# Two of eleven pairs of inner tiles multiplied directly instead of through seven block products

## The chip, the cores and the metric

The kernel runs on one core of a Trainium2 chip. The metric is the device time of one execution in microseconds (us), from a few runs, of which the median is given. TensorE (PE in the rows) multiplies, VectorE (DVE), ScalarE (ACT) and GpSimd (POOL) work element by element, and SyncE (SP) issues the transfers.

## What is computed

A decoder trunk of two layers on 512 tokens of width 1024, all in float32. Every layer is two feed-forward networks (FFNs) around a mixer; the mixers (convolution with sparse attention, short convolution with stick-breaking attention) are not touched by the change. D_FF is 2816.

```python
def _rmsnorm(x, g):
    y = x32 * lax.rsqrt(jnp.mean(x32 * x32, axis=-1, keepdims=True) + RMS_EPS)
    return (y * g.astype(jnp.float32)).astype(x.dtype)

def _swiglu(x, w_in, w_out):
    gate, up = jnp.split(x @ w_in, 2, axis=-1)
    return (jax.nn.silu(gate) * up) @ w_out

def reference(x, ...):
    for layer in range(DEPTH):
        x = x + 0.5 * _swiglu(_rmsnorm(x, ffn1_norm[layer]), ffn1_w_in[layer], ffn1_w_out[layer])
        h = _rmsnorm(x, mix_norm[layer])
        ...
        x = x + y
        x = x + 0.5 * _swiglu(_rmsnorm(x, ffn2_norm[layer]), ffn2_w_in[layer], ffn2_w_out[layer])
    return _rmsnorm(x, final_norm)
```

## The kernel before

The residual `xT` is kept transposed: 8 tiles of 128 channels by 512 tokens. A float32 operand is **split** (`split`, L85) into a high part (ScalarE) and a rest (VectorE, the subtraction), and each product of two split operands is three matmuls (`mm3`, L117 to L120: high x high, high x rest, rest x high). The 2816 inner channels are 22 tiles of 128, taken as 11 **pairs**.

`up(s)` (L248) makes one pair: for each of its two tiles and for gate and up, `load_w` brings 512 KB of weights, splits them (three buffers each for the raw, the high and the rest part), and 24 matmuls of 512 columns fill a PSUM bank (`gu`, four banks with the tag `b`). VectorE multiplies the banks by `rstd`, ScalarE applies Silu, VectorE multiplies gate and up into `hb`. `Seven` (L135) then forms four sums of 256 columns (`ht`) and splits 1792 columns into `ah` and `al`: the seven operands of a Strassen-like 2x2 block product.

`down(c0, n, q, end)` (L270) multiplies n pairs with the output weights for one half (q) of the output tiles. `seven` (L210) loads four weight blocks (`rb`), builds weight sums (`ws`, L235, L236, L238, L242), and calls `product` seven times: a split of the weights, then 6n matmuls of 256 columns into one of the banks `px`, `py`, `pw` (there is one of each), then one update of two output tiles' halves of `xT` by VectorE (`taps`, L277). `px` and `pw` run on through several products of one call, so the update reads a bank between two products into it. `CHUNKS = [3, 3, 3, 2]` gives the number of pairs per call; `ffn` (L289 to L300) puts one `up` between the two halves of a chunk, ahead of need, so that the last chunk (2 pairs) has no `up` left beside it.

When the last chunk has updated four output tiles, `nxt(m)` is called for each: `Norm.add` (L171) makes the next phase's operands `xh` (ScalarE, L91) and `xl` (VectorE, L92), the square (ScalarE) and its running sum `ss` (POOL, the eighth on VectorE). `finish` sums over channels with one-column matmuls (`rs`), computes the inverse root in 12 small VectorE steps, and turns it into `rstd` (`rb`, L206, then ScalarE, L207). The matmuls of the next phase need `xh` and `xl`; its first eviction needs `rstd`. In the last FFN `nf_add` squares the first four tiles and scales them by the final gain, and `last(c, m0)` (L878) does the final norm for each half of the tokens: squares, gains (`xg`), row sums, transposes (`ft`, in banks of the tag `b`), outputs `o`.

The order of instructions on each engine is set when the program is built, by a scheduler with a timeline of its own, which follows the code's order as priority; each engine then runs its list in order.

The program runs FFN, mixer 0, FFN, FFN, mixer 1, FFN. After the first FFN mixer 0 begins with projections (banks `ac`), with windows `xw` that VectorE builds after `rstd`, their split `xwh`, and `cw` matmuls on them. The output projection of mixer 1 (`out_proj`, L362, banks `mo`) makes 24 matmuls, one update and one `nxt` per output tile.

Of the kernel before, what the change touches and what calls it, by code (L numbers as in the profile page):

```python
# [14 lines left out]
P = 128  # L15
# [18 lines left out]

S_11, S_21, S_22, S_T1, S_T3, S_T2, S_T4 = 1, 2, 3, 4, 5, 6, 7

CHUNKS = [3, 3, 3, 2]

FILL = [3, 1, 1, 2, 1, 1, 2, 1]

# [10 lines left out]
def trunk(ctx: ExitStack, tc: tile.TileContext, a: dict, out: bass.AP):  # L51
# [71 lines left out]
    def halves(t):  # L123
        return t.rearrange("p (s t) -> p s t", t=TH)
# [117 lines left out]
        V.tensor_tensor(s[2], s[2], raw["12"], ALU.add)  # L242
        product("3", X, s[2], S_22, False)

    def ffn(norm, w_in, w_out, nxt, ph, last=None):
        act = {}

        def up(s):  # L248

            blk = ph.wide("hb")  # L250
            for r in range(2):
                ps = []
                for gu in range(2):
                    hi, lo = load_w(w_in[2 * s + r, :, gu], KD * P)
                    o = ph.bank("gu")
                    for i, k in enumerate(norm.order):
                        sl = slice(k * P, (k + 1) * P)
# [12 lines left out]
        def down(c0, n, q, end):  # L270
# [18 lines left out]
        todo, done = [], 0  # L289
        for i, n in enumerate(CHUNKS):  # L290
            c0 = sum(CHUNKS[:i])

            while done < min(c0 + n + 1, NP // 2):
                up(done)
                done += 1
            for q in range(2):
                down(c0, n, q, i == len(CHUNKS) - 1)
                if done < NP // 2 and q == 0:
                    up(done)
                    done += 1  # L300

    def proj(norm, src, o, when=nullcontext):
        hi, lo = load_w(src, KD * P)
# [551 lines left out]

    with ffn_phase() as ph:
        n1.finish(lambda s: ph.bank(s, "n"))
        ffn(n1, a["w1_in"][0], a["w1_out"][0], n2.add, ph)
    with Phase(dict(q=8, t=5, p=3, d=4, cc=3), "ss", ss=3, pt=2, po=2, cv=1) as ph:
        n2.finish(lambda s: ph.bank(s, "po"))  # L860
        mixer0(n2, n3.add, ph)
    with ffn_phase() as ph:
        n3.finish(lambda s: ph.bank(s, "n"))
        n4 = Norm(P_N1 + 8)
        ffn(n3, a["w2_in"][0], a["w2_out"][0], n4.add, ph)
        n4.finish(lambda s: ph.bank(s, "n"))
        n5 = Norm(P_NM + 8)
        ffn(n4, a["w1_in"][1], a["w1_out"][1], n5.add, ph)
# [6 lines left out]
    def gain(m):  # L875
        return prm[:, P_NF + m:P_NF + m + 1]

    def last(c, m0):  # L878

        ts = slice(c * TH, (c + 1) * TH)  # L880
        parts = [nf.ss[0][:, ts]]
        xg = [xT[:, m, ts] for m in range(m0)]
        for m in range(m0, KD, 2):
            sq = ctile("sq")
            S.activation(halves(sq), xT[:, m:m + 2, ts], AF.Square)
            parts += [sq[:, :TH], sq[:, TH:]]
            x = ph.tile("xg")
            for j in range(2):
                xg.append(x[:, j * TH:(j + 1) * TH])
                V.tensor_scalar(xg[-1], xT[:, m + j, ts], gain(m + j), None, op0=ALU.mult)  # L890
# [21 lines left out]

    with ffn_phase() as ph:
        n6.finish(lambda s: ph.bank(s, "n"))
        ffn(n6, a["w2_in"][1], a["w2_out"][1], nf_add, ph, last)


def _layout(i):
# [12 lines left out]
    for s, t in (("1", "ffn1"), ("2", "ffn2")):  # L931
# [4 lines left out]
        w = i[f"{t}_w_out"].reshape(2, NP // 2, 2, P, 2, 2, 2, P).transpose(0, 4, 2, 5, 3, 6, 1, 7)  # L936
        cuts = np.split(w, np.cumsum(CHUNKS)[:-1], axis=6)
        w = np.concatenate([x.reshape(2, 2, 2, 2, P, -1) for x in cuts], axis=5)
        d[f"w{s}_out"] = c(w).reshape(2, 2, 4, P, NP * P)
# [76 lines left out]
```

## Time and profile before

| | |
|---|---|
| median of 3 runs | 1998.99 us (1998.45 to 1999.19) |
| the profiled execution, its own time | 1997.97 us |
| its span, first to last instruction | 1995.3 us |
| TensorE busy | 1942.7 us (97%) |
| VectorE busy | 1399.2 us (70%) |
| ScalarE busy | 809.5 us (41%) |
| GpSimd busy | 101.7 us (5%) |
| mean granted TensorE clock, share of full speed | 0.990 |

The profile shows one execution. Matmuls are pipelined and their ends are modelled, so two of them overlap in the rows: the rate is read from starts, not from durations. Full speed of the TensorE clock is 2.4 GHz, the lower level 1.2 GHz. A row of the timeline ends with the idle time of the engine before it and what it waited for.

### The profile page before, as it was taken

Reading aid. Unit: us, or ns where it says so; the run is one execution under the profiler, and the core shown is the slowest. Engines: PE = TensorE matmul, PEld = TensorE weight load, DVE = VectorE, ACT = ScalarE, POOL = GpSimd, SP = SyncE. Lnnn points to the kernel's source line nnn. Section 1 sums busy time; section 2 is a strip of 40 time slices with the busy share of each in tenths; the row PEclk is TensorE's granted clock in tenths of the full one; section 3 lists DMA queues with packets and bytes.
Section 4 is the critical chain, followed back from the end, with each engine's and each line's share of the span. In section 5 each row is a group of like instructions: output and inputs, shape, how many; then the busy total and the mean of one; then the engine's idle time right before and its main releaser. Section 6 shows DMA issues by size and latency. Waiting matters only on the chain.

```text
span 1995.3 us, 26109 instructions
## 1 busy us (share of the span) xinstructions
PE 1942.7 (97%) x10428; PEld 1649.8 (83%) x10428; DVE 1399.2 (70%) x2114; ACT 809.5 (41%) x1173; POOL 101.7 (5%) x109
## 2 busy tenths in 40 slices
PE   8999999889999999999989999998999999999998
PEld 6898988768667888898877888888877888888897
DVE  6575757799976656675786666668758755676667
ACT  5343333436785333333343333334645433333333
POOL 2000000100332100000010000000000010000000
PEclk9999999999999999999989999999999999999999
DMA  6233332222101432333233333331321243232311
GB/s 219 90 98 93 98 102 71 79 87 85 43 1 42 133 102 84 107 90 101 82 91 106 93 101 102 96 91 31 107 74 53 85 135 99 87 110 82 115 45 59
DMA packets 56280, 178.07 MB, mean 89 GB/s; under 512 B 6240, under 2 KB 6624, under 8 KB 56160
## 3 DMA queue, kind: packets, MB, share of 16 engines
q1 hardware_dynamic: 56016, 176.29, 29.1%
q8 instruction: 81, 1.33, 0.3%
q14 instruction: 39, 0.32, 0.0%
q10 hardware_dynamic: 144, 0.14, 0.0%
HBM read 174.30 MB, written 2.10 MB: 88 GB/s over the span
## 4 chain that ended last, share of the span: by engine, by line
PE 93%; DVE 4%; ACT 1%; issue 1%; DMA 1%; SPq 0%; DVEq 0%; ACTq 0%
PE gu L118 16%; PE gu L119 16%; PE gu L120 16%; PE px L118 4%; PE px L119 4%; PE px L120 4%; PE ac L120 3%; PE ac L119 3%; PE ac L118 3%; PE pw L119 2%; PE pw L118 2%; PE pw L120 2%; PE mo L118 2%; PE mo L120 1%; PE mo L119 1%; PE pt L369 1%
## 5 line engine op out<-in xcount | busy, mean ns | idle before, releaser
L118 PE MATMUL gu<-xh,whi 128*128 128x512 f32 x1408 | 548.9, 391 | 11.4 <-ACT whi L88 7.6
L119 PE MATMUL gu<-xl,whi 128*128 128x512 f32 x1408 | 549.5, 390 | 0.1
L120 PE MATMUL gu<-xh,wlo 128*128 128x512 f32 x1408 | 545.2, 390 | 0.0
L88 ACT ACTIVATE whi<-raw 128x1024 fp32r<-128x1024 f32 (+2 forms) x240 | 251.8, 1050 | 563.5 <-PE gu L119 194.0
L89 DVE TENSOR_TENSOR wlo<-raw,whi 128x1024 fp32r<-128x1024 f32 (+2 forms) x240 | 291.0, 1214 | 50.6 <-ACT whi L88 48.7
L118 PEld LDWEIGHTS gu<-xh,whi 128*128 128x128 f32 x1408 | 265.0, 188 | 66.0 <-ACT whi L88 8.4
L120 PEld LDWEIGHTS gu<-xh,wlo 128*128 128x128 f32 x1408 | 264.6, 188 | 55.3
L119 PEld LDWEIGHTS gu<-xl,whi 128*128 128x128 f32 x1408 | 265.0, 188 | 54.2 <-DVE xl L92 1.0
L264 DVE TENSOR_TENSOR u<-gu,rstd 128x512 f32<-128x512 f32 x88 | 60.8, 691 | 262.0 <-PE gu L120 262.0
L88 ACT ACTIVATE whi<-rb 128x768 fp32r<-128x768 f32 (+1 forms) x128 | 101.5, 793 | 295.4 <-PE gu L119 166.3
L118 PE MATMUL px<-ah,whi 128*128 128x256 f32 x704 | 205.8, 292 | 11.6 <-DVE xT L277 9.3
L120 PE MATMUL px<-ah,wlo 128*128 128x256 f32 x704 | 201.2, 286 | 0.4 <-DVE wlo L89 0.4
L119 PE MATMUL px<-al,whi 128*128 128x256 f32 x704 | 200.6, 285 | 0.0
L261 DVE TENSOR_TENSOR g<-gu,rstd 128x512 f32<-128x512 f32 x88 | 60.8, 691 | 151.8 <-PE gu L120 145.7
L118 PEld LDWEIGHTS px<-ah,whi 128*128 128x128 f32 x704 | 134.7, 191 | 24.3 <-issue 8.9
L119 PEld LDWEIGHTS px<-al,whi 128*128 128x128 f32 x704 | 134.9, 192 | 1.0
L120 PEld LDWEIGHTS px<-ah,wlo 128*128 128x128 f32 x704 | 134.6, 191 | 0.7 <-DVE wlo L89 0.7
L120 PE MATMUL ac<-xh,wlo 128*128 128x512 f32 x288 | 113.7, 395 | 4.4 <-DVE wlo L89 4.4
L89 DVE TENSOR_TENSOR wlo<-rb,whi 128x768 fp32r<-128x768 f32 (+1 forms) x128 | 114.8, 897 | 0.8
L119 PE MATMUL ac<-xl,whi 128*128 128x512 f32 x288 | 114.0, 397 | 1.0 <-DVE xl L92 1.0
L118 PE MATMUL ac<-xh,whi 128*128 128x512 f32 x288 | 113.5, 395 | 1.1 <-ACT whi L88 0.9
L118 PE MATMUL pw<-ah,whi 128*128 128x256 f32 x352 | 100.7, 286 | 4.4 <-DVE xT L277 2.2
(307 smaller groups left out, 3179.5 us busy)
## 6 DMA issues: line engine op xcount, KB each, us to landing
raw<-in_w_in SPq DMA_DIRECT2D x174, 512.0 KB, 3.8
rb<-in_w_out SPq DMA_DIRECT2D x96, 384.0 KB, 3.1
raw<-in_cd_a SPq DMA_DIRECT2D x20, 512.0 KB, 3.6
rb<-in_w_out SPq DMA_DIRECT2D x32, 256.0 KB, 2.6
raw<-in_ab_a SPq DMA_DIRECT2D x16, 512.0 KB, 3.6
raw<-in_ab_w_out SPq DMA_DIRECT2D x8, 512.0 KB, 3.6
raw<-in_cd_w_out SPq DMA_DIRECT2D x8, 512.0 KB, 3.5
xT<-in_x SPq DMA_DIRECT2D x8, 256.0 KB, 5.8
```

Of the source, the lines that this page charges most:

```text
L88: S.activation(hi, src, AF.Copy)
L89: V.tensor_tensor(lo, src, hi, ALU.subtract)
L118: PE.matmul(o, wh, xh, start=start, stop=False, **kw)
L119: PE.matmul(o, wh, xl, start=False, stop=False, **kw)
L120: PE.matmul(o, wl, xh, start=False, stop=stop, **kw)
L261: V.tensor_tensor(g, ps[0], rstd, ALU.mult)
L264: V.tensor_tensor(u, ps[1], rstd, ALU.mult)
L369: PE.transpose(pt[:, w:w + P], src[:, OFFQ[i] + t * P:OFFQ[i] + (t + 1) * P], ident)
```

## The change

Only the first nine pairs go through `seven`, in three chunks of three. The last two pairs (four inner tiles, `TAIL = 4`) keep their natural element order and are split as they are (`at`, two tiles of 1024 columns) without sums. After the last chunk `down_tail` makes one output tile after the other: 12 matmuls of 512 columns into a bank `fo` of the tag `b` (four banks, shared with `gu`), one update of `xT`, then `nxt(m)`. One load and split of 1024 columns holds the weights of two output tiles. In the last FFN the eighth output tile is made in two halves of 256 tokens, and `last` squares and scales only this one. The host lays the tail's weights out as `w1_tail` and `w2_tail`. TensorE has 288 matmuls fewer in all: 672 of 256 columns go, 372 of 512 and 24 of 256 come, and 12 row sums go.

```diff
-CHUNKS = [3, 3, 3, 2]
+CHUNKS = [3, 3, 3]
+TAIL = NP - 2 * sum(CHUNKS)
...
-                V.tensor_tensor(o if r else o[:, ::-1], halves(g), halves(u), ALU.mult)
+                tail = s >= sum(CHUNKS)
+                V.tensor_tensor(o if r or tail else o[:, ::-1], halves(g), halves(u), ALU.mult)
+            if tail:
+                h, l = (ph.rtile("at", "act", 1792) for _ in range(2))
+                split(h[:, :1024], l[:, :1024], blk)
+                act[s] = [(h[:, r * T:(r + 1) * T], l[:, r * T:(r + 1) * T]) for r in range(2)]
+                return
...
-            if end and last and q == 1:
-                for c in range(2):
-                    last(c, m0)
-            elif end:
-                for m in range(m0, m0 + 4):
-                    nxt(m)
...
+        def down_tail(m, ts):
+            o = ph.bank("fo")[:, ts]
+            if m // 2 not in ws:
+                ws[m // 2] = load_w(w_tail[m // 2], 2 * TAIL * P)
+            hi, lo = ws[m // 2]
+            for k in range(TAIL):
+                sl = slice((m % 2 * TAIL + k) * P, (m % 2 * TAIL + k + 1) * P)
+                mm3(o, hi[:, sl], lo[:, sl], ops[k][0][:, ts], ops[k][1][:, ts], k == 0, k == TAIL - 1)
+            V.scalar_tensor_tensor(xT[:, m, ts], o, 0.5, xT[:, m, ts], op0=ALU.mult, op1=ALU.add)
+
+        cut = KD - 1 if last else KD
+        for m in range(cut):
+            down_tail(m, slice(0, T))
+            nxt(m)
+        if last:
+            for c in range(2):
+                for m in range(cut, KD):
+                    down_tail(m, slice(c * TH, (c + 1) * TH))
+                last(c, range(cut, KD))
...
-        xg = [xT[:, m, ts] for m in range(m0)]
-        for m in range(m0, KD, 2):
-            sq = ctile("sq")
-            S.activation(halves(sq), xT[:, m:m + 2, ts], AF.Square)
-            parts += [sq[:, :TH], sq[:, TH:]]
...
+        xg = [xT[:, m, ts] for m in range(KD)]
+        for m in ms:
+            sq = ctile("sq")[:, :TH]
+            S.activation(sq, xT[:, m, ts], AF.Square)
+            parts.append(sq)
```

The scheduler's order shows what stands where. On VectorE near the end of the first FFN, before (weight splits `wlo` and sums `ws` of the last chunk, updates of `xT`, norm splits `xl`):

```order
L89 TENSOR_TENSOR wlo_3081<-rb_3067,whi_3080 128x512
L277 SCALAR_TENSOR_TENSOR xT<-px_2911,xT 128x2x256
L89 TENSOR_TENSOR wlo_3098<-rb_3069,whi_3097 128x512
L277 SCALAR_TENSOR_TENSOR xT<-px_2911,xT 128x2x256
L92 SCALAR_TENSOR_TENSOR wlo_3117<-ws_3076,whi_3116 128x512
L242 TENSOR_TENSOR ws_3076<-ws_3076,rb_3069 128x512
L92 SCALAR_TENSOR_TENSOR xl_3038<-xT,prm,xh_3037 128x512
L277 SCALAR_TENSOR_TENSOR xT<-px_3077,xT 128x2x256
L89 TENSOR_TENSOR wlo_3135<-rb_3073,whi_3134 128x512
L277 SCALAR_TENSOR_TENSOR xT<-py_3078,xT 128x2x256
```

And the same place with the change (L94 is L92 before, L315 is the tail's update):

```order
L91 TENSOR_TENSOR wlo_2989<-raw_2986,whi_2988 128x1024
L315 SCALAR_TENSOR_TENSOR xT<-fo_2887,xT 128x512
L94 SCALAR_TENSOR_TENSOR xl_2908<-xT,prm,xh_2907 128x512
L315 SCALAR_TENSOR_TENSOR xT<-fo_2913,xT 128x512
L91 TENSOR_TENSOR wlo_3039<-raw_3036,whi_3038 128x1024
L94 SCALAR_TENSOR_TENSOR xl_2928<-xT,prm,xh_2927 128x512
L315 SCALAR_TENSOR_TENSOR xT<-fo_2935,xT 128x512
L94 SCALAR_TENSOR_TENSOR xl_2956<-xT,prm,xh_2955 128x512
L315 SCALAR_TENSOR_TENSOR xT<-fo_2963,xT 128x512
L91 TENSOR_TENSOR wlo_3135<-raw_3132,whi_3134 128x1024
```

Each output tile now has one update and one norm split, and a weight split stands between every second pair of them; `wlo_3135` is already the next phase's.

On TensorE at the end of the last FFN, before: the row sums `rs` and transposes `ft` of both halves of the tokens, behind the last product:

```order
L120 MATMUL px_16624<-ah_16271,wlo_16734 128x256
L897 MATMUL ft_16799<-cst,xg_16757 128x128
L897 MATMUL ft_16809<-cst,xg_16757 128x128
L185 MATMUL rs_16760<-ones,sq_16755 128x1 x2
L185 MATMUL rs_16760<-ones,ss_16611 128x1
L185 MATMUL rs_16760<-ones,sq_16750 128x1 x2
L185 MATMUL rs_16760<-ones,sq_16755 128x1 x2
L897 MATMUL ft_16799<-cst,xg_16757 128x128
L897 MATMUL ft_16809<-cst,xg_16757 128x128
L185 MATMUL rs_16836<-ones,ss_16611 128x1
```

With the change, the last tile's first half, its transposes and row sums, then the second half:

```order
L122 MATMUL fo_16151<-at_15814,wlo_16130 128x256
L920 MATMUL ft_16197<-cst,xT 128x128 x4
L920 MATMUL ft_16202<-cst,xT 128x128 x2
L920 MATMUL ft_16207<-cst,xT 128x128 x4
L920 MATMUL ft_16212<-cst,xT 128x128 x2
L920 MATMUL ft_16202<-cst,xT 128x128
L920 MATMUL ft_16202<-cst,xg_16167 128x128
...
L187 MATMUL rs_16169<-ones,ss_16148 128x1
L187 MATMUL rs_16169<-ones,sq_16165 128x1
...
L187 MATMUL rs_16247<-ones,ss_16148 128x1
L120 MATMUL fo_16229<-at_15495,whi_16129 128x256
```

The products of the second half moved behind the transposes and row sums of the first; before, the products of both halves were done when the row sums of the second half began.

## Rows read from the trace of the kernel before

**Rows 1.** The page's part on busy time: TensorE.
```profile
PE 1942.7 (97%) x10428; PEld 1649.8 (83%) x10428; DVE 1399.2 (70%) x2114; ACT 809.5 (41%) x1173; POOL 101.7 (5%) x109
```

**Rows 2.** Windows: length, busy time (instructions) per engine, granted clock, DMA share, GB/s.
```profile
354.00:366.00 12.00, 10.42 (x80) 9.57 (x78) 10.76 (x17) 7.76 (x14) 2.99 (x3) 1.00 0.00 1
366.00:374.00 8.00, 5.51 (x36) 5.55 (x37) 7.81 (x11) 3.17 (x5) 1.19 (x1) 0.79 0.00 0
...
1020.00:1034.00 14.00, 10.10 (x42) 9.07 (x43) 11.79 (x16) 3.37 (x5) 1.28 (x1) 0.63 0.32 99
```

**Rows 3.** Timeline, TensorE, first FFN's end: start, duration, instruction, idle before.
```profile
329.94 0.28 PE L118 MATMUL px<-ah,whi 128*128 128x256 f32 x1
...
332.09 0.28 PE L118 MATMUL py<-ah,whi 128*128 128x256 f32 x1
...
368.49 0.55 PE L118 MATMUL px<-ah,whi 128*128 128x256 f32 x1 [2.79 <-DVE xT L277]
...
374.10 0.39 PE L118 MATMUL ac<-xh,whi 128*128 128x512 f32 x1
```

**Rows 4.** Timeline of POOL and VectorE in the same stretch.
```profile
364.22 2.97 POOL L168 TENSOR_TENSOR ss<-ss,sq 128x512 f32<-128x512 f32 x2 [0.96 <-ACT sq L162]
364.33 1.74 DVE L92 SCALAR_TENSOR_TENSOR xl<-xT,prm,xh 128x512 fp32r<-128x512 f32 x1
365.99 1.75 DVE L89 TENSOR_TENSOR wlo<-ws,whi 128x512 fp32r<-128x512 f32 x1
```

**Rows 5.** Groups by line and shape, whole span: count, busy us, mean ns, idle before.
```profile
L89 DVE TENSOR_TENSOR wlo<-raw,whi 128x1024 fp32r<-128x1024 f32 x233 | 284.9, 1223 | 49.2 <-ACT whi L88 47.3 <-DMA raw<-in_w_in 1.6
L88 ACT ACTIVATE whi<-raw 128x1024 fp32r<-128x1024 f32 x233 | 246.8, 1060 | 553.3 <-PE gu L119 194.0 <-issue 159.4 <-PE px L119 81.3
L277 DVE SCALAR_TENSOR_TENSOR xT<-px,xT 128x512 f32<-128x512 f32 x128 | 87.6, 685 | 9.8 <-PE px L120 9.4
L168 POOL TENSOR_TENSOR ss<-ss,sq 128x512 f32<-128x512 f32 x32 | 51.9, 1621 | 73.2 <-ACT sq L162 61.7 <-DVE wlo L89 6.3 <-issue 3.3
L92 DVE SCALAR_TENSOR_TENSOR xl<-xT,prm,xh 128x512 fp32r<-128x512 f32 x48 | 49.3, 1047 | 1.9 <-ACT xh L91 1.7
```

**Rows 6.** Window in the output projection of mixer 1, columns as in rows 2.
```profile
1582.00:1622.00 40.00, 40.00 (x174) 32.47 (x173) 21.24 (x25) 17.56 (x24) 10.87 (x6) 1.00 0.39 128
```

**Rows 7.** Timeline after the first FFN: ScalarE, VectorE, TensorE.
```profile
396.49 0.60 ACT L207 ACTIVATE rstd<-rb 128x512 f32<-128x512 f32 x1 [1.87 <-PE rb L206]
...
408.69 1.22 DVE L89 TENSOR_TENSOR xwh<-xw,xwh 128x1024 fp32r<-128x1024 f32 x1
408.83 0.80 PE L120 MATMUL ac<-xh,wlo 128*128 128x512 f32 x1 [4.44 <-DVE wlo L89]
```

**Rows 8.** Timeline, TensorE, second FFN: first product after `gu`, then the next FFN.
```profile
984.04 0.28 PE L118 MATMUL px<-ah,whi 128*128 128x256 f32 x1
...
1058.44 0.50 PE L118 MATMUL gu<-xh,whi 128*128 128x512 f32 x1 [2.34 <-DVE g L261]
```

**Rows 9.** Timeline, TensorE, third FFN's end and the projections behind it.
```profile
1354.00 0.28 PE L118 MATMUL px<-ah,whi 128*128 128x256 f32 x1
...
1398.11 0.39 PE L118 MATMUL ac<-xh,whi 128*128 128x512 f32 x1
...
1418.38 0.60 PE L206 MATMUL rb<-cst,rcol 128*128 128x128 f32 x4
```

**Rows 10.** Timeline, TensorE and VectorE, last FFN's end and the final norm.
```profile
1937.01 0.28 PE L118 MATMUL px<-ah,whi 128*128 128x256 f32 x1
...
1987.63 0.16 DVE L192 TENSOR_SCALAR rj<-ri 128x2 int32<-128x2 int32 x1
...
1989.39 0.16 DVE L200 SCALAR_TENSOR_TENSOR rcol<-ru,ry 128x2 f32<-128x2 f32 x1
1989.65 1.41 DVE L904 TENSOR_SCALAR o<-ft,rcol 128x512 f32<-128x512 f32 x2
```

More of the change, by code (lines that the diff above doesn't have):

```diff
@@ L243, in seven, with ffn @@
         product("3", X, s[2], S_22, False)
-    def ffn(norm, w_in, w_out, nxt, ph, last=None):
+    def ffn(norm, w_in, w_out, w_tail, nxt, ph, last=None):
         act = {}
@@ L266, in up, with down @@
                 o = halves(blk)[:, 2 * r:2 * r + 2]
-                V.tensor_tensor(o if r else o[:, ::-1], halves(g), halves(u), ALU.mult)
+                tail = s >= sum(CHUNKS)
[5 more added lines that the diff above has]
+                return
             act[s] = Seven(ph.rtile("ah", "act", 1792), ph.rtile("al", "act", 1792), blk, ph.wide("ht"), V)
-        def down(c0, n, q, end):
+        def down(c0, n, q):
             m0 = 4 * q
@@ L281, in down @@
             seven(ph, blocks, n, [act[c0 + k] for k in range(n)], taps)
-            if end and last and q == 1:
-                for c in range(2):
-                    last(c, m0)
-            elif end:
-                for m in range(m0, m0 + 4):
-                    nxt(m)
-        todo, done = [], 0
+        done = 0
         for i, n in enumerate(CHUNKS):
@@ L296, in ffn @@
             for q in range(2):
-                down(c0, n, q, i == len(CHUNKS) - 1)
+                down(c0, n, q)
                 if done < NP // 2 and q == 0:
@@ L300, in ffn @@
                     done += 1
+        ops = sum([act[s] for s in range(sum(CHUNKS), NP // 2)], [])
+        ws = {}
+        def down_tail(m, ts):
[16 more added lines that the diff above has]
+                last(c, range(cut, KD))
     def proj(norm, src, o, when=nullcontext):
@@ L857, in trunk @@
         n1.finish(lambda s: ph.bank(s, "n"))
-        ffn(n1, a["w1_in"][0], a["w1_out"][0], n2.add, ph)
+        ffn(n1, a["w1_in"][0], a["w1_out"][0], a["w1_tail"][0], n2.add, ph)
     with Phase(dict(q=8, t=5, p=3, d=4, cc=3), "ss", ss=3, pt=2, po=2, cv=1) as ph:
@@ L864, in trunk @@
         n4 = Norm(P_N1 + 8)
-        ffn(n3, a["w2_in"][0], a["w2_out"][0], n4.add, ph)
+        ffn(n3, a["w2_in"][0], a["w2_out"][0], a["w2_tail"][0], n4.add, ph)
         n4.finish(lambda s: ph.bank(s, "n"))
         n5 = Norm(P_NM + 8)
-        ffn(n4, a["w1_in"][1], a["w1_out"][1], n5.add, ph)
+        ffn(n4, a["w1_in"][1], a["w1_out"][1], a["w1_tail"][1], n5.add, ph)
     n6 = Norm(P_N2 + 8)
@@ L876, in gain, with last @@
         return prm[:, P_NF + m:P_NF + m + 1]
-    def last(c, m0):
+    def last(c, ms):
         ts = slice(c * TH, (c + 1) * TH)
         parts = [nf.ss[0][:, ts]]
-        xg = [xT[:, m, ts] for m in range(m0)]
-        for m in range(m0, KD, 2):
-            sq = ctile("sq")
-            S.activation(halves(sq), xT[:, m:m + 2, ts], AF.Square)
-            parts += [sq[:, :TH], sq[:, TH:]]
[L887 to L890, printed above, removed]
+        xg = [xT[:, m, ts] for m in range(KD)]
[3 more added lines that the diff above has]
+            parts.append(sq)
+            xg[m] = ph.tile("xg")[:, :TH]
+            V.tensor_scalar(xg[m], xT[:, m, ts], gain(m), None, op0=ALU.mult)
         rsqrt_rows(lambda s: ph.bank(s, "n"), parts, 1.0 / D, RMS_EPS, rcol[:, 2 * c:2 * c + 2], None)
@@ L914, in trunk @@
         n6.finish(lambda s: ph.bank(s, "n"))
-        ffn(n6, a["w2_in"][1], a["w2_out"][1], nf_add, ph, last)
+        ffn(n6, a["w2_in"][1], a["w2_out"][1], a["w2_tail"][1], nf_add, ph, last)
 def _layout(i):
@@ L934, in _layout @@
             c(tiles(w[l]).reshape(2, NP, P, D).transpose(1, 2, 0, 3)) for l in range(2)])
-        w = i[f"{t}_w_out"].reshape(2, NP // 2, 2, P, 2, 2, 2, P).transpose(0, 4, 2, 5, 3, 6, 1, 7)
+        n = NP - TAIL
+        w = i[f"{t}_w_out"][:, :n * P].reshape(2, n // 2, 2, P, 2, 2, 2, P).transpose(0, 4, 2, 5, 3, 6, 1, 7)
         cuts = np.split(w, np.cumsum(CHUNKS)[:-1], axis=6)
         w = np.concatenate([x.reshape(2, 2, 2, 2, P, -1) for x in cuts], axis=5)
-        d[f"w{s}_out"] = c(w).reshape(2, 2, 4, P, NP * P)
+        d[f"w{s}_out"] = c(w).reshape(2, 2, 4, P, n * P)
+        w = i[f"{t}_w_out"][:, n * P:].reshape(2, TAIL, P, KD // 2, 2, P)
+        d[f"w{s}_tail"] = c(w.transpose(0, 3, 2, 4, 1, 5)).reshape(2, KD // 2, P, 2 * TAIL * P)
     ab = i["ab_w_in"][0]
```

## The prediction, made before the change was run

> **What bounds the kernel now.** The page's busy time comes first: TensorE is busy 97% of the span [rows 1]. That is an average, and matmul ends are modelled, so the question is where it runs slower than it can. Two rates answer. In a product the 256-column matmuls start every 0.119 us (18 between the first two rows of [rows 3]); the 512-column ones every 0.23 us (174 in 40.00 us, [rows 6]). The 294 block-product matmuls left after the last `gu` matmul of the first FFN are thus worth 294 x 0.119 = 35.0 us, yet they last from 329.94 to 374.10, 44.2 us [rows 3]. The windows tell why: with no `gu` work left to interleave, VectorE is busy 10.76 of 12 us from 354 and 7.81 of 8 from 366 while TensorE falls to 5.51 of 8 [rows 2], and one product waits 2.79 us for the xT update that frees its bank [rows 3]. After that idle time the granted clock is 0.79 of full speed over the window, which means part of it was at the lower level, 1.2 GHz; at the end of the second FFN it is 0.63 over 14 us [rows 2]. So four stretches of some 45 us, one per FFN, are bound by VectorE and by single `px`, `py`, `pw` banks; the rest by TensorE.
>
> **What the change takes out and puts in, per FFN.** Out go the two 2-pair calls of `seven`: 168 matmuls of 256 columns (20.0 us at 0.119) and on VectorE 14 splits, 8 weight sums and 14 updates of 512 columns. At the 0.685 us of such an update [rows 5], 36 x 0.685 = 24.7 us. In come 96 matmuls of 512 columns: 22.1 us at 0.23. Pure TensorE work therefore **grows by 2.1 us per FFN**. VectorE gets four splits of 1024 columns (4 x 1.223 = 4.9 us) and eight updates (5.5 us) for the 24.7 us. The two last `up` calls also lose their `Seven` sums and splits of 1792 columns for one split of 1024; that lies beside `gu` matmuls and is worth nothing by itself. The other element order at L267 costs nothing: the same instruction, beside `gu` matmuls. Weight bytes stay the same (four transfers of 512 KB for eight of 256 KB), issued behind those of the last `up`, two tiles ahead of use. In the last FFN three more squares, scalings and POOL sums stand beside the `fo` matmuls, and 12 row-sum matmuls go.
>
> The new tail looks like the output projection of the second mixer, which has 24 instead of 12 matmuls per output tile, also several free banks, one update, one norm split and one POOL sum per tile: there TensorE is busy 40.00 of 40 us and VectorE only 21.24 [rows 6]. In the tail a tile has 12 x 0.23 = 2.76 us of TensorE. VectorE needs 0.685 for the update, 1.047 on average for `xl`, and half a weight split, 0.61: **2.34 us** [rows 5]. Next to a POOL addition `xl` and a 512-column split took 1.74 and 1.75 instead of some 0.7 [rows 4]. If both were always caught, a tile would need 0.685 + 1.74 + 0.61 + 0.5 = 3.5 us; the order has two `xl` to a split and POOL is busy 1.62 of 2.76, so I take the average and keep 3.5 for the range. ScalarE's 1.060 us split per two tiles [rows 5] stands ahead of the tile's own work in the order, and three weight buffers let it run two tiles ahead. No `fo` matmul or update has run yet; their prices lie between the rows of 512 columns at 0.23 and, were the clock at its lower level, twice that. I take 0.23: in the new order no wait of TensorE precedes them.
>
> **The four ends, one by one.** From the first product after the last `gu`: the 126 remaining 3-pair matmuls, 15.0 us, then the tail, 22.1: 37.1 us.
> First FFN: 329.94 + 37.1 = 367.0. The order now puts 69 projection matmuls and the row sums before `rb` (82 before the change): 69 x 0.23 + 0.75 = 16.6, so `rb` stands at 383.6 and rstd at 384.1, against 396.49 [rows 7]. What follows is VectorE's window chain in both kernels; it reaches the low half of `xwh` 12.2 us after rstd [rows 7], now at 396.3, done at 397.5. By then both have issued 98 `ac` and two `cw` matmuls; before that point was 408.83 [rows 7]. **Gain 11.3.** The old idle time there is not removed, only brought forward.
> Second FFN: 984.04 + 37.1 = 1021.1; 96 `gu` matmuls, row sums and `rb` (22.1 + 1.3) end at 1044.5. The old order issued all 96 before `rb`, filled the four banks and waited until 1058.44 for the first eviction [rows 8]. Now `rb` comes after 72, so rstd is there at 1040 and the first bank is free by 1042. **Gain 13.9.**
> Third FFN: 1354.00 + 37.1 = 1391.1; 85 `ac` matmuls and the row sums took 1418.38 - 1398.11 = 20.3 us [rows 9]: 1411.4 instead of 1418.38. **Gain 7.0.**
> Last FFN: 1937.01 + 15.0 + 84 x 0.23 + 12 x 0.119 = 1972.7 for the first half of the last tile. The order (shown with the change) puts the second half's 12 matmuls behind the first half's transposes and row sums, and its bank comes free only with an output of the first half. First half: drain 0.3, update 0.7, square 0.6 and row sums 0.8, the rsqrt steps 2.4 (9 starts in 1.76 us, [rows 10], 12 needed), output 0.8: 1978.3. Second half: matmuls 1.4, drain and update 1.0, transposes 2.0 beside the square, row sums 0.3, rsqrt 2.4: last outputs start at 1985.4, against 1989.65 [rows 10]. At the lower clock matmuls and transposes cost 2 to 3 more. **Gain 4.3**, bounds 1 to 6.
> Sum 36.5. The profiled execution took 1997.97 (span 1995.3, 2.7 around it), so 1961.5; it lies 1.0 below the median of the runs, 1998.99, so the forecast is **1962.5 us**. Mixer orders shift by some rows; I count 3 us each way for that.
>
> **Rivals.** (a) VectorE stays the bound in the tail. For it: the 1.74 us beside POOL [rows 4]. At 3.5 us per tile three tails (the last has no `xl`) last 8 x 0.74 = 5.9 longer each: gain 19, 1980 us. Against it: VectorE at half load in [rows 6]. The Trainium skill (GPSIMD Engine Reference, section 1, Specifications) says that POOL's SBUF interfaces are shared with VectorE and contend with instructions that have two SBUF inputs; by that rule the updates, which read PSUM, escape, and the trace agrees with 0.685 us for them on average.
> (b) **Slower**: TensorE's work alone counts, because the waits come back one step later. The place is the norm of the next phase: if the last tile's update, square, POOL sum, row sums and rstd set the moment at which banks come free, shortening the products moves nothing, and the 2.1 us of extra matmul time per FFN is all that is left: 4 x 2.1 = 8.4, 2007 us. It decides once more than 36.5 / 4 = 9.1 us of wait per FFN returns. For it: TensorE's 97% [rows 1], the 4.44 us wait after the first FFN [rows 7]. Against it: the old order leaves four tiles' norm work behind the last products, the new one a single tile's, and the products themselves stand still for VectorE [rows 2, 3].
> The Trainium skill (TensorE: Matmul & The Clock Gate, section "Wait — 56ns, not 53.3ns?") gives a warm back-to-back matmul its columns divided by 2.4 GHz plus about 2.5 ns. By that rule alone the direct form adds 96 x 215.8 - 168 x 109.2 ns, an estimate of 2.4 us per FFN, and the change is slower: rival (b). The trace has 230 and 119 ns instead, and it shows the old products below that rate for a fifth of the stretch.
> (c) The change does less than it says: excluded by the order, which has 288 matmuls fewer.
>
> **How the numbers follow.** Forecast 1962.5 with its own range 1954 to 1972 (orders of the mixers 3, last half 3, small waits up to 2 per end): 0.77. Rival (a), 1972 to 1986: 0.16. Rival (b), about 2007: 0.05. No change: 0.02. The range for 8 in 10 is 1954 to 1976: the forecast's, and the nearer part of (a). A measurement of this kernel tells about 0.2% from no change, 4 us; both (a) and the forecast lie beyond it. Faster 0.93, same 0.02, slower 0.05.
>
> **What would show it.** Per FFN the time from the first product after the last `gu` to the last `fo` should be about 37 us, the `fo` matmuls 0.23 us apart, the granted clock 1.00 there and 0.99 or more over the span; VectorE below full in the tail; its busy time down by some 80 us in total. rstd after the first FFN should come 12 us earlier. Rival (a) would show `fo` or the first projection waiting for VectorE; rival (b) a gap after `rb` or at the first eviction of each phase as long as the time saved. The forecast is wrong if the tail runs at the lower clock or if the mixers' new order opens a wait of its own.

## The result, and the profile after

The changed kernel takes **1965.32 us** (median of 4 runs, 1962.64 to 1970.05), the kernel before beside it 1998.72 (1997.98 to 1999.19): a ratio of **0.9836**, 95% interval 0.9817 to 0.9855, 33.4 us less. The forecast was 1962.5 with a range of 1954 to 1976. The profiled execution of the changed kernel took 1965.56 us (span 1963.8, mean granted clock 0.994), that of the kernel before 1997.97 (span 1995.3, clock 0.990).

From the page of the changed kernel: busy time by engine, and the chain that ended last.

```profile
PE 1930.6 (98%) x10128; PEld 1632.0 (83%) x10128; DVE 1322.0 (67%) x1973; ACT 790.1 (40%) x1129; POOL 104.1 (5%) x112
...
PE 97%; DVE 1%; ACT 1%; issue 0%; DMA 0%; DVEq 0%; SPq 0%; ACTq 0%
```

Against [rows 1] TensorE is busy 12.1 us less and VectorE 77.2 us less. The page counts 300 matmuls fewer and not 288, since each of the 12 row sums that went is two rows of the profile. Windows of the changed kernel: the whole end of the first FFN, its direct part alone, and the end of the last FFN (length, busy us and instructions of PE, PEld, DVE, ACT, POOL, then granted clock, DMA share, GB/s).

```profile
331.50:368.80 37.30, 37.30 (x222) 32.97 (x222) 29.46 (x36) 19.96 (x26) 8.26 (x6) 1.00 0.25 74
...
346.60:368.80 22.20, 22.20 (x97) 17.91 (x97) 15.71 (x20) 12.65 (x18) 8.26 (x6) 1.00 0.39 118
...
1941.00:1964.00 23.00, 11.67 (x79) 10.90 (x77) 9.71 (x33) 5.49 (x10) 2.57 (x2) 0.79 0.24 91
```

Where [rows 2] had VectorE nearly full, TensorE at 5.51 of 8 us and clocks of 0.79 and 0.63, TensorE now runs without a break at the full clock, and VectorE is busy 15.71 of 22.20 us. Only the last FFN's end is still broken, at a mean clock of 0.79. TensorE's timeline: the first product after the last `gu` of each FFN, then the first FFN's last direct matmul with the matmul behind it, and the last FFN's two halves of the eighth output tile.

```profile
331.56 0.28 PE L120 MATMUL px<-ah,whi 128*128 128x256 f32 x1
...
368.84 0.40 PE L122 MATMUL fo<-at,wlo 128*128 128x512 f32 x1
370.11 0.47 PE L120 MATMUL ac<-xh,whi 128*128 128x512 f32 x1 [0.88 <-ACT whi L90]
...
975.01 0.28 PE L120 MATMUL px<-ah,whi 128*128 128x256 f32 x1
...
1330.64 0.28 PE L120 MATMUL px<-ah,whi 128*128 128x256 f32 x1
...
1907.62 0.28 PE L120 MATMUL px<-ah,whi 128*128 128x256 f32 x1
...
1943.64 0.28 PE L122 MATMUL fo<-at,wlo 128*128 128x256 f32 x1
1950.11 0.39 PE L120 MATMUL fo<-at,whi 128*128 128x256 f32 x1 [2.57 <-ACT o L929]
```

With the first products of the kernel before [rows 3, 8, 9, 10] these rows cut the span into stages, each from one FFN's first late product to the next one's. The end of the first FFN with mixer 0 behind it went from 654.10 to 643.45 us, that of the second FFN from 369.96 to 355.63, the third with mixer 1 from 583.01 to 576.98, and the last product stretch to the end of the span from 58.29 to 56.18. Gains: **10.65, 14.33, 6.03 and 2.11**, together 33.1; the stretch up to the first of these products was 1.62 longer in this execution. Each gain compares one execution with one. Four more profiles below (the changed kernel again, both halves first twice, the other banks) have the same instructions up to the last output tile. In all five the second stage lasts 355.5 to 355.6 us and the third 577.0 to 577.1, but the first, with mixer 0 in it, 643.0 to 652.6: its gain of 10.65 is that of a short execution, and in the changed kernel's second profile it is 8.2.

### The profile page after: what moved, and what is told of

It is laid out like the page before. It is cut to its first block, busy times and chain, and to the rows that moved or that the text cites. A ratio compares the mean times of both kernels' runs of the same rounds, so it can differ in the third digit from the quotient of the medians.

```text
span 1963.8 us, 25263 instructions
## 1 busy us (share of the span) xinstructions
PE 1930.6 (98%) x10128; PEld 1632.0 (83%) x10128; DVE 1322.0 (67%) x1973; ACT 790.1 (40%) x1129; POOL 104.1 (5%) x112
## 4 chain that ended last, share of the span: by engine, by line
PE 97%; DVE 1%; ACT 1%; issue 0%; DMA 0%; DVEq 0%; SPq 0%; ACTq 0%
PE gu L120 16%; PE gu L121 16%; PE gu L122 16%; PE px L120 4%; PE px L122 4%; PE px L121 4%; PE ac L120 3%; PE ac L122 3%; PE ac L121 3%; PE pw L122 2%; PE pw L121 2%; PE pw L120 2%; PE fo L120 2%; PE fo L121 2%; PE fo L122 2%; PE mo L121 1%
## 5 line engine op out<-in xcount | busy, mean ns | idle before, releaser
L90 ACT ACTIVATE whi<-raw 128x1024 fp32r<-128x1024 f32 (+2 forms) x256 | 268.9, 1051 | 565.3 <-PE gu L121 188.7
L91 DVE TENSOR_TENSOR wlo<-raw,whi 128x1024 fp32r<-128x1024 f32 (+2 forms) x256 | 312.8, 1222 | 55.0 <-ACT whi L90 51.0
L90 ACT ACTIVATE whi<-rb 128x768 fp32r<-128x768 f32 x96 | 81.4, 848 | 266.5 <-PE gu L121 166.3
L120 PE MATMUL px<-ah,whi 128*128 128x256 f32 x576 | 165.4, 287 | 1.6
L122 PE MATMUL px<-ah,wlo 128*128 128x256 f32 x576 | 163.4, 284 | 0.0
L121 PE MATMUL px<-al,whi 128*128 128x256 f32 x576 | 162.7, 282 | 0.0
L120 PEld LDWEIGHTS px<-ah,whi 128*128 128x128 f32 x576 | 108.8, 189 | 10.4 <-DVE xT L285 4.7
L121 PEld LDWEIGHTS px<-al,whi 128*128 128x128 f32 x576 | 108.7, 189 | 1.2
L122 PEld LDWEIGHTS px<-ah,wlo 128*128 128x128 f32 x576 | 108.6, 188 | 0.0
L91 DVE TENSOR_TENSOR wlo<-rb,whi 128x768 fp32r<-128x768 f32 x96 | 91.7, 955 | 0.8
```

The source lines that it names most:

```text
L90: S.activation(hi, src, AF.Copy)
L91: V.tensor_tensor(lo, src, hi, ALU.subtract)
L120: PE.matmul(o, wh, xh, start=start, stop=False, **kw)
L121: PE.matmul(o, wh, xl, start=False, stop=False, **kw)
L122: PE.matmul(o, wl, xh, start=False, stop=stop, **kw)
```

## The experiments

The runs below are from three chips: the changed kernel again, three pairs, the old last FFN and the first run of the halves on one; both runs with more VectorE work, more banks and less VectorE work on the second; the rest on the third. The kernel before, run beside them on each, showed a wider spread than at first, 1994.8 to 2009.4 us over 46 runs, with a mean clock from 0.992 down to 0.982. Ratios are to those runs, and those of different chips compare only roughly: the same changed kernel has 0.9836 above and 0.9806 below, where the kernel before ran longer beside it (median 2006.29). Medians are compared on one chip where that can be, and what an edit did to a stage is read from the profiles.

**The changed kernel again.** Nothing edited.

> The changed kernel once more, nothing edited: how far its runs lie apart, and the reference for the two runs beside it. The first four lay from 1962.6 to 1970.1 us, while those of the kernel before lay within 1.2. Theory A: the spread comes from the clock granted to TensorE at the start and at the waits that are left; then the longer runs show the lower mean clock (0.990 to 0.995), and the profile shows again a wait of some 2.2 us at the first eviction of the kernel, at 34.7 us, with a lower clock behind it. Rival B: the time at the start was of that one execution; then the start is 1.6 us shorter this time, and the median stands at 1964. Both expect 1963 to 1967.

Measured: 1966.70 us (1964.97 to 1967.37, 5 runs; ratio 0.9806, 0.9779 to 0.9833). The first late product started at 330.89 us this time, 0.7 earlier than at first (theory B put 1.6), and the first eviction's wait was 1.41 us instead of 2.22: nearer to theory B for the start. In the other kernels below (but for three pairs, which shifts the products) that instant lies between 328.7 and 331.7, whichever of the two they were made from, so the 1.6 us are no part of the change. Part of the spread is the clock, as theory A has it: the runs at 0.994 took 1965.0, those at 0.991 and 0.992 took 1966.7 to 1967.4.

**What bounded the old end.** Four variants of the kernel before touch only the last chunk. In the first its last seven products use the four `gu` banks:

```diff
-        X, Y, W = (ph.bank(t, t) for t in ("px", "py", "pw"))
+        X, Y, W = (ph.bank(t, tag or t) for t in ("px", "py", "pw"))
...
-            seven(ph, blocks, n, [act[c0 + k] for k in range(n)], taps)
+            seven(ph, blocks, n, [act[c0 + k] for k in range(n)], taps, "b" if end and q == 1 else None)
```

> The kernel before, where the products of each FFN's last half chunk (the last seven products) take their three banks out of the four that the gu matmuls no longer use, instead of px, py and pw, so that they need not wait for the last updates of the half chunk ahead of them. Theory (VectorE sets the pace): the wait of 2.79 us for an update moves elsewhere; the stretch of 44.2 us after the first FFN shortens by 0 to 2, the time by 0 to 6 us. Rival (single banks set it): the stretch shortens by 3 us or more, and the time by 10 or more.

In the second the last chunk has no low part of its weights:

```diff
-            split(hi, lo, src, sign)
+            if light:
+                S.activation(hi, src, AF.Copy, scale=sign or 1.0)
+                lo = hi
```

> The kernel before, where the last chunk of each FFN (2 pairs) leaves out the low part of its weights: 14 VectorE splits per FFN go, and the third matmul of each product reads the high part, so that TensorE does the same number of matmuls. Theory (VectorE bounded the end): with 14 x 0.7 us less on VectorE the stretch of 44.2 us after the first FFN falls to 36 to 39 us, near the 35.0 that 294 matmuls at 0.119 us are worth, and the time falls by 18 to 32 us: the changed kernel's gain, without its direct products. Rival (the banks or the norm behind it bounded it): the stretch stays above 42 us and the time falls by under 8.

The third has the first one's banks, and two products share one split buffer of 1024 columns:

```diff
+    def pair_of_splits(w):
+        if not spare:
+            spare.append([wsp.tile([P, 1024], F32R, tag=t, name=nm(t)) for t in ("whi", "wlo")])
+            return [x[:, :w] for x in spare[0]]
+        return [x[:, w:2 * w] for x in spare.pop()]
...
+            if end:
+                hi, lo = pair_of_splits(w)
```

> The kernel before with more banks in the last half chunk (as in the run with more banks alone) and with room for six products' split weights instead of three in the last chunk (two products of 512 columns share one buffer of 1024); VectorE's work is unchanged. Theory J (two limits of the old end lie close together: VectorE's own work, some 41 us per FFN, and the turnaround through three split buffers and single banks, some 44): the waits for ScalarE's splits go, VectorE stays full, and the stretch that lasted 44.0 us before and 41.1 with more banks lasts 40 to 42 us; the time is that with more banks, 1989 to 1996. Rival T (the turnaround alone bounded it): the stretch falls to 36 to 38 us, the time to 1970 to 1980.

The fourth is the third without the low parts.

> The same, and the last chunk also leaves out the low part of its weights (14 VectorE splits per FFN fewer; the third matmul reads the high part). Theory J: both limits are gone and TensorE's own work is left, so the stretch after the first FFN lasts 35.5 to 38 us, and the time falls by 15 to 30 us, to 1970 to 1984. Rival: a third limit (the updates of xT, which must follow one another in the banks and in xT) holds it at 41 us or more.

The window from the first late product to the last product of the first FFN, columns as above. The kernel before:

```profile
330.00:374.00 44.00, 38.46 (x295) 36.84 (x294) 41.74 (x60) 21.24 (x32) 4.17 (x3) 0.96 0.11 31
```

More banks:

```profile
331.20:372.30 41.10, 37.06 (x294) 35.48 (x294) 39.66 (x58) 21.37 (x33) 4.33 (x3) 1.00 0.12 33
```

Less VectorE work:

```profile
329.60:374.00 44.40, 37.16 (x294) 35.32 (x294) 33.48 (x47) 22.05 (x33) 4.17 (x3) 1.00 0.12 35
```

More banks and split buffers:

```profile
331.00:370.30 39.30, 36.11 (x295) 35.18 (x294) 38.80 (x60) 20.27 (x31) 2.27 (x2) 1.00 0.20 59
```

All three:

```profile
331.10:366.80 35.70, 35.34 (x295) 34.98 (x294) 29.66 (x42) 18.58 (x28) 1.29 (x1) 1.00 0.16 43
```

The same 294 matmuls take 44.0, 41.1, 44.4, 39.3 and 35.7 us. Taking 8 us off VectorE alone brings nothing: the stretch stays at 44.4 with VectorE idle for a quarter of it, so the expectation that VectorE by itself bounded the end is refuted, and its rival holds. The timeline of that run shows the other limit, on ScalarE (ACT) and TensorE:

```profile
357.20 0.28 PE L120 MATMUL px<-ah,whi 128*128 128x256 f32 x1
357.51 0.63 ACT L225 ACTIVATE whi<-rb 128x512 fp32r<-128x512 f32 x1 [1.84 <-PE px L120]
...
358.20 0.39 PE L118 MATMUL py<-ah,whi 128*128 128x256 f32 x1 [0.72 <-ACT whi L225]
```

A split waits until a product has let go of its buffer, and the next product waits for that split: TensorE stands idle five times in the stretch for 0.60 to 0.72 us, beside waits of 0.78, 1.27 and 1.73 us for updates that free a bank. With more banks alone the stretch shortened by 2.9 us, between the two expectations. With banks and buffers widened it lasts 39.3 us, just under theory J's 40 to 42 and above rival T's 36 to 38, and VectorE is busy 38.80 of it: now VectorE is the bound. Only both together reach 35.7, next to the 35.0 that the matmuls are worth at 0.119. **Theory J holds**, with the first stretch a little shorter than it put: two limits lay close together, VectorE's work at some 39 us and the turnaround through banks and split buffers at 44.

The times followed only in part: 1993.39 us with more banks (before 1998.68; ratio 0.9974, 0.9957 to 0.9990), 2004.60 with less VectorE work (1.0013, 0.9993 to 1.0033), 1989.18 with banks and buffers (0.9947, 0.9923 to 0.9972; before 1998.69), 1981.27 with all three (0.9894, 0.9856 to 0.9932). The last has a shorter product stretch than the changed kernel, 35.7 against 37.3 us, and still takes longer: 15 us by the medians of two chips, 10 to 11 at like clocks (1975.65 us at 0.993, the changed kernel 1965.0 at 0.994). Its timeline on TensorE, the waits for norm work behind the products of the first three FFNs:

```profile
371.36 0.62 PE L119 MATMUL ac<-xl,whi 128*128 128x512 f32 x1 [3.37 <-DVE xl L92]
...
1052.33 0.50 PE L118 MATMUL gu<-xh,whi 128*128 128x512 f32 x1 [2.34 <-DVE g L276]
...
1388.11 0.50 PE L119 MATMUL ac<-xl,whi 128*128 128x512 f32 x1 [3.37 <-DVE xl L92]
```

After the first and the third FFN a projection waits 3.37 us for norm splits, after the second the first eviction is waited for as in the kernel before [rows 8], and after the first FFN rstd starts 63.8 us after the last `gu` (66.8 in the kernel before, 56.1 in the changed one). From late product to late product the second FFN takes 359.6 us and the third with mixer 1 581.1, the changed kernel 355.6 and 577.0. Shorter products alone leave the wait for the four tiles' norm work that stands behind them; the changed kernel, which finishes one output tile after the other, has none of these three waits. That the order does this, and no other part of the direct form, is argued from the rows: no run has direct products in the old order.

**More VectorE work**, eight additions of 512 columns per FFN: in the kernel before among the updates of the last chunk, in the changed one behind the update of each output tile.

```diff
+                if end and m in "1265":
+                    V.tensor_tensor(halves(dumb), x, x, ALU.add)
...
+            V.tensor_tensor(dumb[:, ts], xT[:, m, ts], xT[:, m, ts], ALU.add)
```

> The kernel before, with eight more VectorE additions of 512 columns (0.685 us each, 5.5 us per FFN) between the updates of each FFN's last chunk; nothing reads their results. Theory (VectorE bounded the old end): each FFN's end grows by 4 to 5.5 us; the stretch from the first product after the last gu to the first ac matmul after the first FFN goes from 44.2 to 48 to 50 us, and the time by 16 to 20 us. Rival (the single banks, or TensorE's own work, bounded it): the additions fall into idle time of VectorE and the stretch grows by under 1.5 us, the time by under 5.

> The changed kernel, with one more VectorE addition of 512 columns (0.685 us) per output tile of the tail, eight per FFN, whose result nothing reads: the same load as in the run beside it. Theory (TensorE bounds the new end, with 2.06 us of VectorE in a tile's 2.80): a tile has 0.74 us to spare, the fo matmuls stay 0.2335 us apart, and the time grows by 0 to 3 us. Rival (a) of the forecast (VectorE is at its limit there too): 8 x 0.6 us per FFN, 14 to 19 us more.

In the kernel before: 2023.24 us (2012.88 to 2027.93; ratio 1.0119, 1.0086 to 1.0151), beyond the theory's 16 to 20. The window of the first FFN's end, and TensorE's longest wait in it:

```profile
331.70:377.80 46.10, 38.92 (x295) 37.09 (x294) 45.20 (x66) 21.26 (x32) 4.23 (x3) 0.96 0.10 29
```

```profile
372.04 0.36 PE L119 MATMUL px<-ah,whi 128*128 128x256 f32 x1 [3.50 <-DVE xT L278]
```

VectorE is full for 45.20 of 46.10 us; the stretch grew by 2.1 us, less than the 4 to 5.5 expected. rstd came 72.7 us after the last `gu` instead of 66.8: behind the products a projection waits 2.09 us for `xh`, and the granted clock is 0.87 from 377 to 404 us, where the kernel before has 1.00 from 373 to 400. Much of the 25 us comes with the clock: this profiled run has a mean of 0.978, and the run at 0.988 took 2012.88, some 14 us more than the kernel before at 0.988 (1997.1 to 1999.5). Whether the additions lowered the clock is not shown.

In the changed kernel: 1974.08 us (1969.85 to 1982.15; ratio 0.9880, 0.9848 to 0.9912), against 1966.70 for the changed kernel on the first chip. VectorE's groups in its direct part (count, busy us, mean ns, idle before), and the matmul behind that part on TensorE:

```profile
L95 DVE SCALAR_TENSOR_TENSOR xl<-xT,prm,xh 128x512 fp32r<-128x512 f32 x6 | 7.6, 1264 | 0.2
L92 DVE TENSOR_TENSOR wlo<-raw,whi 128x1024 fp32r<-128x1024 f32 x5 | 6.1, 1219 | 0.6 <-ACT whi L91 0.6
L317 DVE TENSOR_TENSOR dumb<-xT 128x512 f32<-128x512 f32 x6 | 5.0, 825 | 0.2
L316 DVE SCALAR_TENSOR_TENSOR xT<-fo,xT 128x512 f32<-128x512 f32 x6 | 4.1, 684 | 1.2 <-PE fo L123 1.1
```

```profile
370.79 0.76 PE L121 MATMUL ac<-xh,whi 128*128 128x512 f32 x1 [3.78 <-DVE xw L484]
```

The first and last direct matmuls stand 22.17 us apart, as without the additions: the matmuls did not slow down, and rival (a) is refuted where the forecast placed it. But VectorE's spare time is used up, and its backlog is paid behind the direct part: the `ac` wait there grows from 0.88 to 3.78 us (the releaser in the row, a clearing of `xw`, is what stands behind that backlog). The expected 0 to 3 us were too few. The two runs at clock 0.993 took 1970 us, 3 to 5 over the changed kernel, those at 0.985 and 0.987 more.

**Three pairs direct.**

```diff
-CHUNKS = [3, 3, 3]
+CHUNKS = [3, 3, 2]
...
-            if m // 2 not in ws:
-                ws[m // 2] = load_w(w_tail[m // 2], 2 * TAIL * P)
+            if m not in ws:
+                ws[m] = load_w(w_tail[m // 2][:, m % 2 * TAIL * P:(m % 2 + 1) * TAIL * P], TAIL * P)
```

> Three pairs of inner tiles are multiplied directly instead of two: the chunks are 3, 3 and 2 pairs, an output tile has 18 matmuls, and its weights are loaded and split for each tile (768 columns). If TensorE alone bounds the tail now, a pair costs what its matmuls cost: 48 of 512 columns at 0.2335 us, 11.2, for 84 of 256 at 0.119, 10.0: 1.2 us more per FFN and 5 us more in all (3 to 8), about 1970. Rival: VectorE or the weights' splits still bound the tail, so that taking one more pair out of the sums and splits pays again; then the time is the same or lower, 1960 to 1965. A time over 1975 would mean that the shorter last chunk or its transfers opened a wait.

Measured: 1988.80 us (1984.37 to 1992.47; ratio 0.9919, 0.9888 to 0.9949), 22 us more than two pairs. Of the 18.9 us between the profiled spans (the changed kernel's is the second one, 1965.6) 4.8 are the matmuls, as expected (the eight tiles of 18 matmuls last 33.6 us). The larger part stands at the shorter chunk, on TensorE in the first FFN:

```profile
280.21 0.36 PE L120 MATMUL px<-ah,whi 128*128 128x256 f32 x1 [1.06 <-DVE xT L285]
...
313.44 0.36 PE L120 MATMUL px<-ah,whi 128*128 128x256 f32 x1 [1.06 <-DVE xT L285]
```

Each FFN has two such waits and one of 0.57 us for a split, 10.8 us in all: a call with two pairs has products of 12 matmuls, 1.43 us, and the waits show that this is too short for the turnaround even with `gu` matmuls beside it. So three pairs per call matter, and two direct pairs are better than three.

**The last FFN.** First with the old end in this FFN alone; then with the matmuls of both halves of the eighth tile ahead of the final norm; then with the second half's transposes in other banks besides.

```diff
+        ffn(n6, a["w2_in"][1], a["w2_out"][1], a["w2_tail"][1], nf_add, ph, last, CHUNKS + [TAIL // 2])
...
             for c in range(2):
                 for m in range(cut, KD):
                     down_tail(m, slice(c * TH, (c + 1) * TH))
+            for c in range(2):
                 last(c, range(cut, KD))
...
-                pt = ph.bank("ft")
+                pt = ph.bank("ft", [None, "px", "py", "pw"][len(turns)] if c else None)
```

> The first three FFNs take the last two pairs directly, the last FFN takes them through seven block products as in the kernel before, with the old final norm. Theory: the ends pay one by one, and the last FFN paid only 2.1 us by the two profiles; so this kernel is 2 us slower than the changed one (0 to 4), 1967.5. By the forecast's own term it would be 4.3 us slower. Rival: the last FFN's direct form is a loss that something else hid; then this kernel is faster than the changed one.

> In the last FFN the 12 matmuls of the last tile's second half go ahead of the final norm of the first half, instead of behind its transposes and row sums; nothing else is edited. Theory: the wait of 2.57 us for an output of the first half and the lower clock behind it (fo 0.21 us apart instead of 0.12) are what the last FFN gained less than forecast; they go, and the kernel is 2.5 to 4 us faster than the changed one, about 1961.5. Rival: the last half's chain of row sums, small VectorE steps and outputs sets the end, and delaying the first half's norm by 1.4 us of matmuls gives it back; then the difference is under 1 us.

> The changed kernel with the last tile's second half ahead of the final norm, once more: 1957 to 1962 us, 5 to 8 below the changed kernel's 1966.7. If the 7 us of the first comparison were half luck of the clock, the median lies at 1962 to 1964.

> The same, and the transposes of the second half of the tokens in the final norm go into px, py, pw and one bank of the tag b, instead of waiting 2.09 us for an output of the first half to leave its bank. Theory: the transposes then run beside the first half's norm at the full clock, the last outputs follow rcol at once, and the kernel ends 1.5 to 3 us earlier than with the halves alone, at 1956 to 1958. Rival: the last rcol sets the end, and the gain is under 1 us.

The old end: 1967.04 us (1966.72 to 1967.67), against 1966.70 for the changed kernel beside it. From the first late product to the end of the span it takes 57.7 us, against 56.2 changed and 58.3 before: the direct form as written is worth 0 to 2 us in this FFN, not 4.3.

Both halves first: **1959.46** us (1957.35 to 1968.48; 0.9779, 0.9753 to 0.9805) beside 1966.70, and again **1960.21** (1957.51 to 1968.57; 0.9799, 0.9773 to 0.9826). From the first late product to the end it takes 51.1 us (1905.88 to 1957.0), 5.0 less than the changed kernel. All but two of the 12 runs lie between 1957.4 and 1961.8; the two at 1968.5 have a clock of 0.989. The rest of the difference of medians, some 2 us, lies ahead of the edit, where both kernels have the same instructions, and is not the edit's. What limits the end is, on TensorE and VectorE:

```profile
1948.10 0.16 DVE L202 SCALAR_TENSOR_TENSOR rcol<-ru,ry 128x2 f32<-128x2 f32 x1
...
1949.10 0.47 PE L921 MATMUL ft<-cst,xT 128*128 128x128 f32 x1 [2.09 <-ACT o L930]
...
1950.86 0.16 DVE L202 SCALAR_TENSOR_TENSOR rcol<-ru,ry 128x2 f32<-128x2 f32 x1
```

The transposes of the second half wait for an output of the first, and so does its norm on VectorE, which runs its list in order: between the sixth and the seventh of the second half's small steps stand two outputs of the first half and an `xg`, so these steps start 1.70 us apart instead of 0.2.

With the other banks: 1958.67 us (1958.10 to 1959.96; 0.9788, 0.9763 to 0.9813), not to be told from the halves alone; the stretch to the end is 51.8 us, 0.7 longer. The expected 1.5 to 3 us did not come: the same wait of 2.09 us is still there, at 1948.85, since one of the four banks is still taken from the shared four, and the second half's rcol, the rival's mechanism, starts at 1950.61, 46.0 us after the first late product (45.0 with the halves alone). Both versions beat the two kernels compared here.

## Why the prediction was right

**What bounds it.** The stretches and the gain were located rightly, and the time of the new one is nearly exact: 126 products and 96 direct matmuls were to take 37.1 us and take 37.3 to their last start; the direct matmuls start 0.233 us apart, where 0.23 was put. Of the cause half was named. The prediction gave VectorE's load as the reason and mentioned single banks; the three buffers for split weights and ScalarE's 0.63 us between two products were missing. The runs show that taking VectorE's load away alone shortens nothing (44.4 us), that banks and buffers bring 4.7 us, and that VectorE's load then brings 3.6. The number did not suffer, because the direct form eases all three at once: one split serves 24 matmuls of 512 columns instead of 12 of 256, and four banks take turns. That is read from the two forms; no run takes their shares in the changed kernel apart.

**VectorE in the new part.** Groups of the changed kernel from 346 to 369 us:

```profile
L170 POOL TENSOR_TENSOR ss<-ss,sq 128x512 f32<-128x512 f32 x5 | 7.5, 1492 | 6.0 <-ACT sq L164 6.0
L91 DVE TENSOR_TENSOR wlo<-raw,whi 128x1024 fp32r<-128x1024 f32 x5 | 6.1, 1226 | 1.2 <-ACT whi L90 1.2
...
L94 DVE SCALAR_TENSOR_TENSOR xl<-xT,prm,xh 128x512 fp32r<-128x512 f32 x7 | 5.2, 750 | 3.2 <-ACT xh L93 3.2
L315 DVE SCALAR_TENSOR_TENSOR xT<-fo,xT 128x512 f32<-128x512 f32 x7 | 4.9, 693 | 2.3 <-PE fo L122 2.2
```

A tile costs VectorE 0.69 + 0.75 + 0.61 = 2.05 us of its 2.80, where 2.34 was put: `xl` takes 0.75 us and not the average 1.05 of [rows 5]. Six of the seven do run beside a POOL addition, but each of them starts before it, and what slows `xl` is to start behind one (the last section has the rows). Rival (a) was nearer than its chance says: with one more addition per tile three of six `xl` start behind a POOL addition again, and VectorE needs 0.68 + 0.83 + 1.26 + 0.61 = 3.38 us on average, more than a tile lasts. That the order of starts came out well was not foreseen: here the prediction had luck.

**The four terms.** First FFN 11.3 put, 10.65 measured, which is partly luck, since a second profile gives 8.2; as forecast, the idle time in mixer 0 only came forward (4.25 us before a `cw` matmul at 401.00, 4.44 before in [rows 7]), and rstd stands at 387.45, 9 us earlier instead of 12; 1.6 of the difference is the late start. Second FFN 13.9 put, 14.33 measured: the wait of 2.34 us for the first eviction [rows 8] is gone. Third FFN 7.0 put, 6.03 measured: `rb` starts 53.7 us after the first late product, 3.7 earlier than worked out, but because the order has 67 `ac` matmuls ahead of it instead of the 85 assumed; they stand behind it, and rstd moves while the work does not. Last FFN 4.3 put, 2.11 measured, within its bounds of 1 to 6. The wait of 2.57 us of the second half's matmuls for an output of the first was in the sum; three other things were short in it. The first half's matmuls end some 0.4 us later than put. From there to the freed bank it takes 6.4 us and not 5.6, for on TensorE 16 transposes stand ahead of the first half's row sums. And the second half takes 8.1 us to its last outputs and not 7.1: the prediction put it at full speed (and named 2 to 3 us more for the lower level), but soon after the wait its matmuls start twice as far apart, and the 12 take 2.10 us instead of 1.4:

```profile
1950.81 0.32 PE L122 MATMUL fo<-at,wlo 128*128 128x256 f32 x1
1950.93 0.41 PE L120 MATMUL fo<-at,whi 128*128 128x256 f32 x1
1951.14 0.41 PE L121 MATMUL fo<-at,whi 128*128 128x256 f32 x1
```

The window behind shows the granted clock at its lower level:

```profile
1951.00:1954.00 3.00, 3.00 (x16) 3.00 (x16) 0.78 (x2) 0.42 (x1) 0.00 (x0) 0.50 0.89 343
```

The last outputs start at 1958.18, 50.6 us after the first late product; 48.4 were put. With the halves in the other order the products of the second half no longer wait, and the term becomes 7.

**Rival (b)** had the right place but not the right size: waits do return behind the products when only the products are shortened (3.37 us, the three edits together), and the direct order avoids them by ending one tile at a time.

**The sum.** 33.1 us of stages against 36.5 put; 33.4 between the medians.

## What to carry to other kernels

When a stretch is slow and one engine in it is full, take that engine's load away in a variant before naming it as the cause: here that alone changed nothing until buffers and banks were widened too. Less matmul time can be worth less than matmuls that are long enough for the splits and updates around them: the direct form has 2.1 us more of it per FFN by the prediction's sum and came out ahead. Results that are finished one by one leave less norm work behind the last. Put independent matmuls ahead of a chain of small steps at the end of a kernel, not between its halves.

## What the runs showed of the hardware

**The granted clock differs between executions of the same instructions.** The changed kernel and the one with both halves first have word for word the same lists on all engines up to the last output tile. Window 544 to 576 us in mixer 0; the changed kernel, twice:

```profile
544.00:576.00 32.00, 29.65 (x147) 19.70 (x146) 25.83 (x86) 25.59 (x66) 8.22 (x16) 0.95 0.00 1
```

```profile
544.00:576.00 32.00, 29.64 (x141) 20.02 (x140) 24.65 (x81) 23.91 (x61) 8.24 (x16) 0.89 0.00 1
```

Both halves first, its first profile:

```profile
544.00:576.00 32.00, 29.64 (x118) 19.51 (x117) 22.43 (x73) 22.39 (x55) 7.62 (x16) 0.74 0.00 1
```

The clock is 0.95, 0.89 and 0.74 there, behind the same waits of TensorE (1.38 to 1.39 us at 536 in all three). Over whole runs it decides most of the spread: on the second of the chips the kernel before took 1994.8 us at 0.991 and 2009.2 at 0.983, and 0.008 of 2000 us is 16. By the same measure part of the change's gain is clock: the span times the mean clock is 1975 us before and 1952 after, 23 of the 31.5 us, and the other 8 are what the lower level cost more before. This is an estimate: the means are rounded to 0.001, 2 us, and count idle time as well.

**Neighbours on SBUF.** In the direct part `xl` took 750 ns in the changed kernel and 1264 with one more VectorE addition per tile, while the update that reads PSUM stayed at 693 and 684. This agrees with what the Trainium skill says (GPSIMD Engine Reference, section 1, Specifications): POOL contends with VectorE instructions that have two SBUF inputs. The rows show more: which of the two starts first. In the changed kernel `xl` starts 0.11 us before a POOL addition; with one more addition per tile it starts 0.38 us behind one:

```profile
360.12 0.75 DVE L94 SCALAR_TENSOR_TENSOR xl<-xT,prm,xh 128x512 fp32r<-128x512 f32 x1
360.23 1.79 POOL L170 TENSOR_TENSOR ss<-ss,sq 128x512 f32<-128x512 f32 x1 [1.54 <-ACT sq L164]
```

```profile
352.34 1.61 POOL L171 TENSOR_TENSOR ss<-sq,sq 128x512 f32<-128x512 f32 x1 [328.25 <-ACT sq L165]
352.72 1.78 DVE L95 SCALAR_TENSOR_TENSOR xl<-xT,prm,xh 128x512 fp32r<-128x512 f32 x1
```

Over the whole kernel before, the 15 `xl` of 48 that start while a POOL addition runs take 1.18 to 1.78 us, the other 33 take 0.73 to 0.75; in the changed kernel 6 take 1.19 to 1.79 and 42 take 0.74 to 0.75. In these rows the collision thus depends on the order of starts, not on how much the two engines run.
